# Two-layer hybrid trunk: other order of the first products at each seam, a split norm tile, one operation for the S5 lags, zero matmuls in front

## The chip, the cores and the metric

The kernel runs on one core of a Trainium2 chip. Its time is the device time of one execution in microseconds (us); what is given is the median of three timed executions, 1226.21 us (they were 1229.82, 1226.21 and 1224.89). Engines: PE is TensorE (matrix products and transposes), DVE is VectorE, ACT is ScalarE, POOL is GpSimd, SP is SyncE (here it only issues loads).

## The reference, cut to what matters

256 tokens of width 1024 go through two layers. Each layer is two SwiGLU blocks of hidden width 2816 around a token mixer, then a gated per-layer embedding. Mixer AB of layer 0 is an SSD (16 heads) beside an S5 (64 groups of 16 channels, 64 states each); mixer CD of layer 1 is HGRN2 beside GLA.

```python
for i in range(DEPTH):
    x = layer_norm(a * x + 0.5 * swiglu(x, gate[i, 0], up[i, 0], down[i, 0]), ...)   # LN0 / LN3
    x = layer_norm(a * x + mix(x, ...), ...)                                          # LN1 / LN4
    x = layer_norm(a * x + 0.5 * swiglu(x, gate[i, 1], up[i, 1], down[i, 1]), ...)   # LN2 / LN5
    x = x + sigmoid(x @ ple_gate[i]) * (p[i] @ ple_proj[i])                           # PLE0 / PLE1
```

All of it is float32.

## The kernel before, in words

Products are made in a reduced float32 form on TensorE. Each operand is split in two: `h` is the operand cast (on ACT), `l` is what is left of it (operand minus `h`, on DVE). A product is then three matmuls, `h·wh`, `h·wl` and `l·wh`, added in PSUM. Weights come in units of 1 MB (`Weights.unit`, L45). SP issues the load of a unit into one of two buffers `wst`; ACT casts its halves to `wh_N_0` and `wh_N_1` (L61), DVE subtracts to get `wl_N_0` and `wl_N_1` (L62). A unit serves four blocks k of 128 inputs and 512 outputs, so it feeds 12 matmuls for each of the two token tiles t0 and t1. One product over all 1024 inputs takes two units (kh = 0 and 1) and 24 matmuls for each tile.

The stages follow one another: SwiGLU f00, LN0, mixer AB, LN1, SwiGLU f01, LN2, PLE0, f10, LN3, mixer CD, LN4, f11, LN5, PLE1. In a SwiGLU (`ffn_body`, L198) `gate_up(f)` makes 512 columns (256 of gate, 256 of up) for both tiles, ACT takes the silu, DVE multiplies, PE transposes the result (`ht_f`, L215), and `down` adds to the four accumulators.

A seam is the place where one stage's output becomes the next one's input. At a layer norm (`layer_norm`, L117) DVE scales the tile in two halves of 512 columns (`x_ln`, L138), PE transposes each half in four 128 x 128 pieces into one PSUM tile (`tp_ln`, L142), and `split_xT` (L107) has ACT cast that to `xh` (L112) and DVE subtract to get `xl` (L113). The first product behind a seam is run with `tile_major=True` (`run_tiles`, L163): all 24 matmuls of t0 before those of t1, and for each unit first `h·wh, h·wl` of its four blocks and then its four `l·wh`. This holds for gate_up(0) of every SwiGLU and for the first projection of each mixer (`pj_u` in AB, `pj_hq` in CD). f00's input comes straight from memory: four loads on ACT's queue (L1340), t0's two halves before t1's.

While f00 runs, the parameters of the S5 are also made, one batch b of eight at a time (`s5_params`, L500), mostly on DVE. In `rest` (L534) PE makes the lag matrices in PSUM (`s5k`); DVE writes 16 of the 64 columns of `s5K` (L552) and ACT copies the other 48 (L554), then POOL sends `s5K` to memory.

What sets the order: each engine runs its instructions in one fixed order. That order is chosen when the program is built, by a scheduler that plays the instructions on a timeline of its own; it may put an instruction ahead of ones written earlier. `behind` (L90) adds the demand that an instruction stand after given ones on its engine: `g.w.behind[n]` names the last split of a seam, behind which the casts and subtractions of unit n must stand. PSUM tiles come from a pool in which the tag "tr" (transposes, S5 matrices) has two buffers and "mm" (products) has two. A dependency between two writes or a write and a read of one PSUM tile is kept for the tile as a whole.

Of the kernel before, what the change touches and what calls it, by code (L numbers as in the profile page):

```python
# [8 lines left out]
F32 = mybir.dt.float32  # L9
# [24 lines left out]
def f32(ap):  # L34
    return ap.bitcast(F32)
# [62 lines left out]
def new_xT(g, name):  # L98
    return [g.xt.tile([P, KT, NTOK], F32R, tag=f"x{p}", name=f"x{p}_{name}") for p in "hl"]
# [4 lines left out]
    return [x[:, k, t * P:(t + 1) * P] for x in xT]  # L104


def split_xT(g, t, half, src, xT):  # L107

    nc = g.nc
    s = slice(4 * half, 4 * half + 4)  # L110
    h, l = (x[:, s, t * P:(t + 1) * P] for x in xT)
    a = nc.scalar.copy(h, src)  # L112
    b = nc.vector.tensor_tensor(l, src, f32(h), op=ALU.subtract)  # L113
    g.anchors = a.ins, b.ins


def layer_norm(g, n, t, acc, coef, xT):  # L117

    nc = g.nc
    name = f"ln{n}_{t}"  # L120
    r = g.lnp.tile([P, D], F32, tag="ln_r", name=f"r_{name}")
    st = g.small.tile([P, 2, 6], F32, tag="ln_st", name=f"st_{name}")
    half = [slice(512 * h, 512 * h + 512) for h in range(2)]
    for h in range(2):
        s = half[h]
        op = nc.vector.scalar_tensor_tensor(r[:, s], acc[h], coef, g.x[t][:, s], op0=ALU.mult, op1=ALU.add)
        if t:
            behind(g, op, g.scaled)
        nc.vector.bn_stats(st[:, h, :], r[:, s])
    mv = g.small.tile([P, 2], F32, tag="ln_mv", name=f"mv_{name}")  # L130
    nc.vector.bn_aggr(mv, st.rearrange("p a b -> p (a b)"))
    rstd = rsqrt(g, mv[:, 1:2], 1, EPS / (ALPHA * ALPHA), 1.0, name)
    x = g.xp.tile([P, D], F32, tag=f"x{t}", name=f"x_{name}")
    for h in range(2):
        s = half[h]
        nc.vector.scalar_tensor_tensor(r[:, s], r[:, s], mv[:, 0:1], g.grow[n][0][:, s], op0=ALU.subtract,
                                       op1=ALU.mult)
        op = nc.vector.scalar_tensor_tensor(x[:, s], r[:, s], rstd, g.grow[n][1][:, s], op0=ALU.mult, op1=ALU.add)  # L138
        g.scaled = (op.ins,)
        tp = g.ps.tile([P, 4, P], F32, tag="tr", name=f"tp_{name}_{h}", bufs=2)  # L140
        for k in range(4):
            nc.tensor.transpose(tp[:, k, :], x[:, (4 * h + k) * P:(4 * h + k + 1) * P], g.ident)  # L142
        split_xT(g, t, h, tp, xT)
    g.x[t] = x
    g.w.behind[g.w.at + 1 + t] = g.anchors

# [16 lines left out]
def run_tiles(g, ps, xT, tile_major=False):  # L163

    nc = g.nc

    def part(kh, t, pieces):
        mms = []
        for j in range(4):
            k = 4 * kh + j  # L170
            wh, wl = pieces[j // 2]
            c = slice(512 * (j % 2), 512 * (j % 2) + 512)
            h, l = of_tile(xT, t, k)
            mms += [(h, wh[:, c]), (h, wl[:, c]), (l, wh[:, c])]
        if tile_major:
            mms = [m for i, m in enumerate(mms) if i % 3 < 2] + mms[2::3]
        for i, (x, w) in enumerate(mms):
            nc.tensor.matmul(ps[t], x, w, start=kh == 0 and i == 0, stop=kh == 1 and i == len(mms) - 1)  # L178

    if tile_major:  # L180
        units = [g.w.unit() for kh in range(2)]
        for t in range(NT):
            for kh in range(2):
                part(kh, t, units[kh])
        return
    for kh in range(2):
# [11 lines left out]
def ffn_body(g, name, ln, hooks, hp, wx):  # L198
# [2 lines left out]

    def gate_up(f):
        ps = [g.ps.tile([P, 512], F32, tag="mm", name=f"gu_{name}_{f}_{t}", bufs=2) for t in range(NT)]
        run_tiles(g, ps, g.xT, tile_major=f == 0)
        return ps

    def hidden(f, ps):
# [72 lines left out]
def ple(g, i, pp, out):  # L280
# [16 lines left out]
    def finish(t, c):  # L297
        step = 256 if last and t == NT - 1 and c else 512
        for s in (slice(i, i + step) for i in range(512 * c, 512 * c + 512, step)):
            a = acc[t][c][:, s.start - 512 * c:s.stop - 512 * c]  # L300
            sg = g.pp.tile([P, step], F32, bufs=2, tag="ple_sg", name=f"sg_ple{i}_{t}_{s.start}")
            nc.scalar.activation(sg, a, AF.Tanh, scale=0.5)
            nc.vector.scalar_tensor_tensor(sg, sg, 1.0, pp[t][:, s], op0=ALU.add, op1=ALU.mult)
            nc.vector.scalar_tensor_tensor(xn[t][:, s], sg, 0.5, xn[t][:, s], op0=ALU.mult, op1=ALU.add)
            if last:
                nc.sync.dma_start(out[t * P:(t + 1) * P, s], xn[t][:, s])
        if last:
            return
        tp = g.ps.tile([P, 4, P], F32, tag="tr", name=f"tp_ple{i}_{t}_{c}", bufs=2)
        for k in range(4):  # L310
            nc.tensor.transpose(tp[:, k, :], xn[t][:, (4 * c + k) * P:(4 * c + k + 1) * P], g.ident)
        split_xT(g, t, c, tp, xT)

    for kh in range(2):
        units[0][kh] = g.w.unit()
# [184 lines left out]
def s5_params(g, b, half):  # L500
# [34 lines left out]
    def rest():  # L535
# [242 lines left out]
def ssd_steps(g, pool, raw):  # L778
# [529 lines left out]
def tile_trunk(ctx: ExitStack, tc: tile.TileContext, xnat, xTd, pT, lnr, colsd, cstd, abrow, abdt, s5bc, cdlr, cdgu,  # L1308
# [23 lines left out]
    g.s5T = [g.dram.tile([P, 4, 64], F32, tag=f"s5T{b}", name=f"s5T{b}") for b in range(NB)]  # L1332
    g.perm = [[g.dram.tile([512, NTOK] if n == "u" else [32, 16, NTOK], F32, tag=f"{n}{c}", name=f"{n}dram{c}")
               for c in range(2)] for n in "uy"]
    g.xT = new_xT(g, "in")
    for t in range(NT):
        xs = g.lnp.tile([P, KT, P], F32, tag="ln_r", name=f"xin_{t}")
        for h in range(2):
            s = slice(4 * h, 4 * h + 4)
            nc.scalar.dma_start(xs[:, s], xTd[t][:, s])  # L1340
            split_xT(g, t, h, xs[:, s], g.xT)

    def load_constants():
        cs = g.const.tile([P, cstd.shape[1]], F32, tag="cst", name="cs")
# [92 lines left out]
def constants():  # L1437
# [4 lines left out]
    for lv in range(7):  # L1442
# [101 lines left out]
```

## Time and profile before

| | |
|---|---|
| median of three timed executions | 1226.21 us |
| profiled execution, its own time | 1226.01 us |
| its span, first to last instruction | 1224.2 us |
| PE busy | 1189.6 us (97%) |
| DVE busy | 852.3 us (70%) |
| ACT busy | 588.5 us (48%) |
| mean granted TensorE clock | 0.994 of full speed |
| chain of waits | PE 67%, DVE 10%, DMA 2%, ACT 2% |

The profiled execution lasts 1.8 us longer than its span, and lies 0.2 us under the median, so times worked out against it need no correction. Stages by time in the span: f00 to 218, AB to 442, f01 to 632, PLE0 to 662, f10 to 852, CD to 1000, f11 to 1195, PLE1 to the end. In the rows, a line such as `PE L178 MATMUL gu_f<-wh,xh_in` is the product into `gu_f` of line 178; a trailing bracket gives how long the engine idled before the instruction and which work ended the wait.

### The profile page before, as it was taken

The page shows a single profiled execution, that of the slowest core. Times are in us where ns is not written, and L with a number is a line of the kernel's source. Part 1 is how long each engine was busy: PE and PEld are TensorE (multiplying, and loading weights), DVE is VectorE, ACT ScalarE, POOL GpSimd, SP SyncE. Part 2 cuts the span into 40 slices and gives each one's busy share as a digit, 9 for nine tenths or more (in the row PEclk, how much of TensorE's full clock was granted, in tenths as well). Part 3 has the DMA queues.
Part 4 walks back from the last instruction along what each step waited for, and adds up shares of the span by engine and source line. Part 5 has one row for each costly group of instructions (what it writes and reads, how often), then busy time and mean ns, then how long its engine had stood idle before and what let it go on. Part 6 is the DMA issues. An engine that isn't in the chain of part 4 may idle for free.

```text
span 1224.2 us, 17248 instructions
## 1 busy us (share of the span) xinstructions
PE 1189.6 (97%) x6786; PEld 987.4 (81%) x6786; DVE 852.3 (70%) x1352; ACT 588.5 (48%) x870; POOL 73.2 (6%) x126
## 2 busy tenths in 40 slices
PE   8999999999999999999999999999999999999998
PEld 6887777798878878888887888887888868888886
DVE  6999874779999675554576545456689876555566
ACT  5644443444666434444434444443575535444434
POOL 0011112120212000000000000000100100000000
PEclk9999999899999999999999999999999999999999
DMA  7567667587744546555526555554633327555532
GB/s 282 207 228 257 223 205 290 211 271 239 198 122 143 192 153 226 201 176 194 203 95 240 196 190 188 185 193 158 241 113 128 104 99 254 176 202 174 203 138 103
DMA packets 44609, 232.74 MB, mean 190 GB/s; under 512 B 9680, under 2 KB 10352, under 8 KB 20848
## 3 DMA queue, kind: packets, MB, share of 16 engines
q1 hardware_dynamic: 30672, 206.06, 48.5%
q0 software_dynamic: 4688, 14.16, 3.7%
q10 hardware_dynamic: 9168, 11.42, 2.9%
q8 instruction: 53, 0.87, 0.3%
q14 instruction: 28, 0.23, 0.1%
HBM read 219.56 MB, written 12.06 MB: 189 GB/s over the span
## 4 chain that ended last, share of the span: by engine, by line
PE 67%; DVE 10%; DMA 2%; ACT 2%; issue 1%; ACTq 0%; DVEq 0%
PE gu_f L178 29%; PE acc_f L72 5%; PE acc_f L70 5%; PE acc_f L71 5%; DVE wl L62 3%; DMA wst<-in_wall_dram 1%; PE acc_ab L72 1%; PE acc_ab L70 1%; PE acc_ab L71 1%; PE ht_f L215 1%; PE pj_u L178 1%; PE pj_hg L178 1%; PE pj_gr L178 1%; PE pj_hi L178 1%; PE pj_gv L178 1%
## 5 line engine op out<-in xcount | busy, mean ns | idle before, releaser
L62 DVE TENSOR_TENSOR wl<-wst,wh 128x1024 fp32r<-128x1024 f32 (+1 forms) x378 | 453.0, 1217 | 258.2 <-ACT wh L61 251.0
L61 ACT CAST wh<-wst 128x1024 fp32r<-128x1024 f32 (+1 forms) x378 | 385.9, 1045 | 349.2 <-PE acc_f L72 104.6
L70 PE MATMUL acc_f<-wh,hh_f 128*128 128x512 f32 x352 | 137.3, 391 | 1.9 <-ACT wh L61 1.4
L71 PE MATMUL acc_f<-wl,hh_f 128*128 128x512 f32 x352 | 137.5, 392 | 0.0
L72 PE MATMUL acc_f<-wh,hl_f 128*128 128x512 f32 x352 | 135.2, 392 | 0.0
L70 PEld LDWEIGHTS acc_f<-wh,hh_f 128*128 128x128 f32 x352 | 66.1, 188 | 15.8 <-ACT wh L61 1.6
L178 PE MATMUL gu_f<-wh,xh_in 128*128 128x512 f32 x176 | 71.9, 413 | 6.0 <-ACT wh L61 6.0
L72 PEld LDWEIGHTS acc_f<-wh,hl_f 128*128 128x128 f32 x352 | 66.1, 188 | 13.7
L71 PEld LDWEIGHTS acc_f<-wl,hh_f 128*128 128x128 f32 x352 | 66.1, 188 | 13.5
L178 PE MATMUL gu_f<-wh,xh_ple 128*128 128x512 f32 x176 | 70.8, 402 | 2.6 <-ACT xh_ple L112 2.6
L178 PE MATMUL gu_f<-wh,xh_ab 128*128 128x512 f32 x176 | 69.8, 396 | 0.5 <-ACT xh_ab L112 0.5
L178 PE MATMUL gu_f<-wl,xh_in 128*128 128x512 f32 x176 | 70.2, 402 | 0.0
L178 PE MATMUL gu_f<-wl,xh_ab 128*128 128x512 f32 x176 | 68.8, 391 | 1.3 <-DVE wl L62 1.3
L178 PE MATMUL gu_f<-wh,xh_cd 128*128 128x512 f32 x176 | 69.9, 397 | 0.0
L178 PE MATMUL gu_f<-wl,xh_ple 128*128 128x512 f32 x176 | 69.6, 396 | 0.0
L178 PE MATMUL gu_f<-wl,xh_cd 128*128 128x512 f32 x176 | 68.8, 391 | 0.7 <-DVE wl L62 0.7
L211 ACT ACTIVATE sg_f<-gu_f 128x256 f32<-128x256 f32 x88 | 33.7, 383 | 69.1 <-PE gu_f L178 67.8
L178 PE MATMUL gu_f<-wh,xl_ab 128*128 128x512 f32 x176 | 66.9, 391 | 0.0
L178 PE MATMUL gu_f<-wh,xl_cd 128*128 128x512 f32 x176 | 66.8, 391 | 0.0
L178 PE MATMUL gu_f<-wh,xl_ple 128*128 128x512 f32 x176 | 66.7, 391 | 0.0
L178 PE MATMUL gu_f<-wh,xl_in 128*128 128x512 f32 x176 | 66.6, 392 | 0.0
L212 DVE TENSOR_TENSOR sg_f<-sg_f,gu_f 128x256 f32<-128x256 f32 x88 | 36.8, 418 | 27.8 <-ACT sg_f L211 27.7
(469 smaller groups left out, 2348.9 us busy)
## 6 DMA issues: line engine op xcount, KB each, us to landing
wst<-in_wall_dram SPq DMA_DIRECT2D x185, 1024.0 KB, 4.8
row<-in_lnr_dram SPq DMA_DIRECT2D x12, 512.0 KB, 6.4
s5d<-s5pk POOLq DMA_DIRECT2D x8, 704.0 KB, 4.3
tab<-s5d ACTq DMA_DIRECT2D x8, 384.0 KB, 4.7
Q<-s5d ACTq DMA_DIRECT2D x8, 320.0 KB, 4.5
wst<-in_wall_dram SPq DMA_DIRECT2D x4, 512.0 KB, 6.7
s5d<-s5W POOLq DMA_DIRECT2D x8, 256.0 KB, 2.5
W<-s5d ACTq DMA_DIRECT2D x8, 256.0 KB, 4.0
```

The costliest lines, as they stand in the source:

```text
L61: ops = [nc.scalar.copy(wh[:, c], src[:, c])]
L62: ops.append(nc.vector.tensor_tensor(wl[:, c], src[:, c], f32(wh[:, c]), op=ALU.subtract))
L70: nc.tensor.matmul(out, xh, wh, start=first, stop=False)
L71: nc.tensor.matmul(out, xh, wl, start=False, stop=False)
L72: nc.tensor.matmul(out, xl, wh, start=False, stop=last)
L178: nc.tensor.matmul(ps[t], x, w, start=kh == 0 and i == 0, stop=kh == 1 and i == len(mms) - 1)
L211: nc.scalar.activation(sg, ps[t][:, 0:256], AF.Silu)
L212: nc.vector.tensor_tensor(sg, sg, ps[t][:, 256:512], op=ALU.mult)
L215: nc.tensor.transpose(tp[:, k, :], sg[:, k * P:(k + 1) * P], g.ident)
```

## The change: what it does

1. Start. Eleven matmuls of a zeroed 128 x 128 tile with itself (128 x 512 out, results not used) stand in front of the first product. x is loaded half by half (t0 and t1 of the first half, then of the second). f00's first gate_up is no longer tile-major.
2. Seams. The tile-major order is now, for each tile: `h·wh, h·wl` of blocks 0 to 3, `h·wh` of blocks 4 to 7, all eight `l·wh`, and last `h·wl` of blocks 4 to 7. This holds for f01, f10 and f11 and for `pj_u` and `pj_hq`.
3. Layer norm. For the first half of t0 the scaling (`x_ln`), the transposes and the split run in two pieces of 256 columns, in the same PSUM tile as before.
4. S5. All 64 lag columns are made by one DVE operation (the constant `fold` grows from 16 to 64 columns); the eight ACT copies go.
5. PLE0. The splits of the units 100 and 101 (the first two of f10) must stand behind the split of the second half of t0 and of t1.

```diff
+START_MMS = 11
...
-def split_xT(g, t, half, src, xT):
+def split_xT(g, t, half, src, xT, part=slice(0, 4)):
-    s = slice(4 * half, 4 * half + 4)
+    s = slice(4 * half + part.start, 4 * half + part.stop)
...
-        op = nc.vector.scalar_tensor_tensor(x[:, s], r[:, s], rstd, g.grow[n][1][:, s], op0=ALU.mult, op1=ALU.add)
-        g.scaled = (op.ins,)
         tp = g.ps.tile([P, 4, P], F32, tag="tr", name=f"tp_{name}_{h}", bufs=2)
-        for k in range(4):
-            nc.tensor.transpose(tp[:, k, :], x[:, (4 * h + k) * P:(4 * h + k + 1) * P], g.ident)
-        split_xT(g, t, h, tp, xT)
+        n = 4 if t or h else 2
+        for k0 in range(0, 4, n):
+            c = slice((4 * h + k0) * P, (4 * h + k0 + n) * P)
+            op = nc.vector.scalar_tensor_tensor(x[:, c], r[:, c], rstd, g.grow[ln][1][:, c], op0=ALU.mult, op1=ALU.add)
+            g.scaled = (op.ins,)
+            for k in range(k0, k0 + n):
+                nc.tensor.transpose(tp[:, k, :], x[:, (4 * h + k) * P:(4 * h + k + 1) * P], g.ident)
+            split_xT(g, t, h, tp[:, k0:k0 + n, :], xT, slice(k0, k0 + n))
...
-        if tile_major:
-            mms = [m for i, m in enumerate(mms) if i % 3 < 2] + mms[2::3]
...
         for t in range(NT):
-            for kh in range(2):
-                part(kh, t, units[kh])
+            mms = [[], [], []]
+            for k in range(KT):
+                wh, wl = units[k // 4][k % 4 // 2]
+                c = slice(512 * (k % 2), 512 * (k % 2) + 512)
+                h, l = of_tile(xT, t, k)
+                mms[0].append((h, wh[:, c]))
+                if k < 4:
+                    mms[0].append((h, wl[:, c]))
+                else:
+                    mms[2].append((h, wl[:, c]))
+                mms[1].append((l, wh[:, c]))
+            mms = sum(mms, [])
+            for i, (x, w) in enumerate(mms):
+                nc.tensor.matmul(ps[t], x, w, start=i == 0, stop=i == len(mms) - 1)
...
-        run_tiles(g, ps, g.xT, tile_major=f == 0)
+        run_tiles(g, ps, g.xT, tile_major=f == 0 and name != "f00")
...
         split_xT(g, t, c, tp, xT)
+        if c:
+            g.w.behind[g.w.at + 1 + t] = g.anchors
...
-        nc.vector.scalar_tensor_tensor(K[:, 48:64], g.cst("fold"), g.cols("s5d")[:, b:b + 1], kp[:, 0:16], op0=mul,
-                                       op1=add)
-        nc.scalar.copy(K[:, 64:112], kp[:, 16:64])
+        nc.vector.scalar_tensor_tensor(K[:, 48:112], g.cst("fold"), g.cols("s5d")[:, b:b + 1], kp, op0=mul, op1=add)
...
+    busy = g.const.tile([P, P], F32R, tag="busy", name="busy")
+    nc.vector.memset(f32(busy), 0.0)
+    ps = g.ps.tile([P, 4, P], F32, tag="tr", name="busy_ps", bufs=2)
+    for i in range(START_MMS):
+        nc.tensor.matmul(ps, busy, bc(busy, 1, 4), start=True, stop=True)
     g.xT = new_xT(g, "in")
-    for t in range(NT):
-        xs = g.lnp.tile([P, KT, P], F32, tag="ln_r", name=f"xin_{t}")
-        for h in range(2):
+    xs = [g.lnp.tile([P, KT, P], F32, tag="ln_r", name=f"xin_{t}") for t in range(NT)]
+    for h in range(2):
+        for t in range(NT):
             s = slice(4 * h, 4 * h + 4)
-            nc.scalar.dma_start(xs[:, s], xTd[t][:, s])
-            split_xT(g, t, h, xs[:, s], g.xT)
+            nc.scalar.dma_start(xs[t][:, s], xTd[t][:, s])
+            split_xT(g, t, h, xs[t][:, s], g.xT)
```

How the built order moves is shown at three places. First ACT behind LN3, from the casts of t0 on. `tp_ln3_0_0` is the transposed first half of t0, `tp_ln3_0_1` the second; `wh_133_*` is the second unit of `pj_hq`, `nws_glr` a small weight that comes by a load of its own. Before:

```order
L112 CAST xh_f10_7743<-tp_ln3_0_0_7784 128x4x128
L112 CAST xh_f10_7743<-tp_ln3_0_1_7793 128x4x128
L61 CAST wh_133_0_7881<-wst_133_7879 128x1024
L61 CAST wh_133_1_7885<-wst_133_7879 128x1024
L1238 DMA gup_8124<-in_cdgu_dram 32x256
L595 CAST nws_glr_8102<-nw_glr_8100 128x8x16
L1055 COPY ev_hq_0_7937<-pj_hq_0_7867 128x512
```

and now:

```order
L113 CAST xh_f10_7758<-tp_ln3_0_0_7798 128x2x128
L113 CAST xh_f10_7758<-tp_ln3_0_1_7810 128x4x128
L62 CAST wh_133_0_7899<-wst_133_7897 128x1024
L62 CAST wh_133_1_7903<-wst_133_7897 128x1024
L1252 DMA gup_8142<-in_cdgu_dram 32x256
L609 CAST nws_glr_8120<-nw_glr_8118 128x8x16
L113 CAST xh_f10_7758<-tp_ln3_0_0_7798 128x2x128
L1069 COPY ev_hq_0_7955<-pj_hq_0_7885 128x512
```

The cast of the first half has become two of 256 columns. The second of them stands behind both `wh_133` casts and `nws_glr`, five rows after the first. At LN0, LN1 and LN4 it likewise stands behind both `wh` casts of the second unit (34, 62 and 151); `nws` is in between at LN3 alone.

Next PE at the same place, from the transposes of t0 on. `wh_132_*` and `wl_132_*` are the first unit of `pj_hq`, which serves blocks 0 to 3. Before:

```order
L142 MATMUL tp_ln3_0_0_7784<-cs_217,x_ln3_0_7781 128x128 x4
L142 MATMUL tp_ln3_0_1_7793<-cs_217,x_ln3_0_7781 128x128 x4
L178 MATMUL pj_hq_0_7867<-wh_132_0_7871,xh_f10_7743 128x512
L178 MATMUL pj_hq_0_7867<-wl_132_0_7872,xh_f10_7743 128x512
L178 MATMUL pj_hq_0_7867<-wh_132_0_7871,xh_f10_7743 128x512
L178 MATMUL pj_hq_0_7867<-wl_132_0_7872,xh_f10_7743 128x512
L178 MATMUL pj_hq_0_7867<-wh_132_1_7875,xh_f10_7743 128x512
L178 MATMUL pj_hq_0_7867<-wl_132_1_7876,xh_f10_7743 128x512
L178 MATMUL pj_hq_0_7867<-wh_132_1_7875,xh_f10_7743 128x512
L178 MATMUL pj_hq_0_7867<-wl_132_1_7876,xh_f10_7743 128x512
L178 MATMUL pj_hq_0_7867<-wh_132_0_7871,xl_f10_7744 128x512 x2
```

and now:

```order
L146 MATMUL tp_ln3_0_0_7798<-cs_231,x_ln3_0_7796 128x128 x2
L146 MATMUL tp_ln3_0_1_7810<-cs_231,x_ln3_0_7796 128x128 x4
L198 MATMUL pj_hq_0_7885<-wh_132_0_7889,xh_f10_7758 128x512
L198 MATMUL pj_hq_0_7885<-wl_132_0_7890,xh_f10_7758 128x512
L198 MATMUL pj_hq_0_7885<-wh_132_0_7889,xh_f10_7758 128x512
L198 MATMUL pj_hq_0_7885<-wl_132_0_7890,xh_f10_7758 128x512
L146 MATMUL tp_ln3_0_0_7798<-cs_231,x_ln3_0_7796 128x128 x2
L198 MATMUL pj_hq_0_7885<-wh_132_1_7893,xh_f10_7758 128x512
L198 MATMUL pj_hq_0_7885<-wl_132_1_7894,xh_f10_7758 128x512
L198 MATMUL pj_hq_0_7885<-wh_132_1_7893,xh_f10_7758 128x512
L198 MATMUL pj_hq_0_7885<-wl_132_1_7894,xh_f10_7758 128x512
L198 MATMUL pj_hq_0_7885<-wh_133_0_7899,xh_f10_7758 128x512 x2
```

Two of the four transposes of the first half now stand behind four products. In the program as built they also wait for DVE's subtraction `xl` of the first piece, since both pieces share one PSUM tile; the four products after them need the second piece of `xh`.

Last ACT between PLE0 and f10. `tp_ple0_T_H` is the transposed half H of tile T, `wh_100_*` and `wh_101_*` the first two units of f10. Before:

```order
L61 CAST wh_100_0_6441<-wst_100_6439 128x1024
L302 ACTIVATE sg_ple0_0_512_6366<-acc_ple0_0_1_6227 128x512
L61 CAST wh_100_1_6445<-wst_100_6439 128x1024
L61 CAST wh_101_0_6521<-wst_101_6519 128x1024
L112 CAST xh_ple0_6230<-tp_ple0_0_0_6304 128x4x128
L112 CAST xh_ple0_6230<-tp_ple0_1_0_6315 128x4x128
L302 ACTIVATE sg_ple0_1_512_6401<-acc_ple0_1_1_6229 128x512
L61 CAST wh_101_1_6525<-wst_101_6519 128x1024
L112 CAST xh_ple0_6230<-tp_ple0_0_1_6370 128x4x128
L61 CAST wh_102_0_6555<-wst_102_6553 128x1024
```

and now:

```order
L316 ACTIVATE sg_ple0_0_512_6381<-acc_ple0_0_1_6242 128x512
L113 CAST xh_ple0_6245<-tp_ple0_0_0_6319 128x4x128
L113 CAST xh_ple0_6245<-tp_ple0_1_0_6330 128x4x128
L316 ACTIVATE sg_ple0_1_512_6416<-acc_ple0_1_1_6244 128x512
L113 CAST xh_ple0_6245<-tp_ple0_0_1_6385 128x4x128
L62 CAST wh_100_0_6456<-wst_100_6454 128x1024
L62 CAST wh_100_1_6460<-wst_100_6454 128x1024
L113 CAST xh_ple0_6245<-tp_ple0_1_1_6420 128x4x128
L62 CAST wh_101_0_6536<-wst_101_6534 128x1024
L62 CAST wh_101_1_6540<-wst_101_6534 128x1024
```

Before, three of the four `wh` casts of the units 100 and 101 stand ahead of the first `xh_ple`; now three `xh_ple` stand ahead of all of them, and `wh_100` follows the split of t0's second half.

## Rows read from the trace of the kernel before

**Rows 1.** The page's first part: busy us, share of the span, instructions.

```profile
PE 1189.6 (97%) x6786; PEld 987.4 (81%) x6786; DVE 852.3 (70%) x1352; ACT 588.5 (48%) x870; POOL 73.2 (6%) x126
```

**Rows 2.** Waits of PE: line waited for, us in total, times, longest.

```profile
PE gu_f L178 <- ACT wh L61: 6.0, 1, 6.0
PE tp_ln L142 <- DVE x_ln L138: 3.5, 3, 1.7
PE gu_f L178 <- ACT xh_ple L112: 2.6, 1, 2.6
PE gu_f L178 <- DVE wl L62: 2.1, 2, 1.3
PE pj_z L178 <- DVE bc L817: 1.9, 1, 1.9
PE ht_f L215 <- ACT s5K L554: 1.8, 2, 1.5
...
PE pj_hq L178 <- DVE wl L62: 1.6, 1, 1.6
```

**Rows 3.** Windows: length, busy us by engine, PEclk, DMA share, GB/s.

```profile
21.10:50.00 28.90, 28.90 (x133) 23.81 (x132) 24.34 (x71) 22.30 (x35) 0.00 (x0) 1.00 0.66 223
...
222.00:245.00 23.00, 22.07 (x119) 19.04 (x119) 16.73 (x23) 14.68 (x19) 1.58 (x2) 0.87 0.71 256
...
665.00:668.50 3.50, 3.50 (x10) 2.76 (x9) 3.50 (x6) 1.48 (x3) 0.00 (x0) 0.52 0.29 122
```

**Rows 4.** Timeline of the start: start us, us, engine, line, operation [idle before].

```profile
6.03 0.79 PE L178 MATMUL gu_f<-wh,xh_in 128*128 128x512 f32 x1 [6.03 <-ACT wh L61]
...
10.45 0.63 PE L178 MATMUL gu_f<-wh,xh_in 128*128 128x512 f32 x1
...
10.87 0.63 PE L178 MATMUL gu_f<-wl,xh_in 128*128 128x512 f32 x1
...
15.21 1.16 DVE L62 TENSOR_TENSOR wl<-wst,wh 128x1024 fp32r<-128x1024 f32 x1
...
21.11 0.48 PE L178 MATMUL gu_f<-wh,xh_in 128*128 128x512 f32 x1
```

**Rows 5.** Timeline of the S5 wait inside f00.

```profile
105.80 0.23 DVE L552 SCALAR_TENSOR_TENSOR s5K<-cs,lc,s5k 128x16 f32<-128x16 f32 x1
105.94 0.42 DVE L218 TENSOR_TENSOR hl_f<-ht_f,hh_f 128x256 fp32r<-128x256 f32 x1
...
106.36 0.33 PE L215 MATMUL ht_f<-cs,sg_f 128*128 128x128 f32 x1 [1.49 <-ACT s5K L554]
```

**Rows 6.** Timeline of the first product behind LN1, PE.

```profile
450.77 1.03 PE L142 MATMUL tp_ln<-cs,x_ln 128*128 128x128 f32 x8
```

**Rows 7.** Timeline between PLE0 and f10, ACT and PE.

```profile
663.03 1.04 ACT L61 CAST wh<-wst 128x1024 fp32r<-128x1024 f32 x1 [3.42 <-DMA wst<-in_wall_dram]
663.98 1.07 ACT L112 CAST xh_ple<-tp_ple 128x512 fp32r<-128x512 f32 x2
...
664.61 0.50 PE L178 MATMUL gu_f<-wh,xh_ple 128*128 128x512 f32 x1 [2.61 <-ACT xh_ple L112]
```

**Rows 8.** Timeline behind LN3, PE and ACT.

```profile
853.51 0.50 PE L178 MATMUL pj_hq<-wh,xh_f 128*128 128x512 f32 x1 [0.24 <-ACT xh_f L112]
...
858.37 0.50 PE L178 MATMUL pj_hq<-wl,xh_f 128*128 128x512 f32 x1 [1.60 <-DVE wl L62]
...
861.22 1.04 PE L142 MATMUL tp_ln<-cs,x_ln 128*128 128x128 f32 x8
...
853.83 2.01 ACT L61 CAST wh<-wst 128x1024 fp32r<-128x1024 f32 x2
857.30 0.30 ACT L595 CAST nws_glr<-nw_glr 128x128 fp32r<-128x128 f32 x1 [1.45 <-DMA nw_glr<-in_cdlr_dram]
```

**Rows 9.** Timeline behind LN4, PE.

```profile
1001.71 0.50 PE L178 MATMUL gu_f<-wh,xh_cd 128*128 128x512 f32 x1
...
1009.04 1.29 PE L142 MATMUL tp_ln<-cs,x_ln 128*128 128x128 f32 x8 [0.26 <-DVE x_ln L138]
```

More of the change, by code (lines that the diff above doesn't have):

```diff
@@ L114, in split_xT, with layer_norm @@
     g.anchors = a.ins, b.ins
-def layer_norm(g, n, t, acc, coef, xT):
+def layer_norm(g, ln, t, acc, coef, xT):
     nc = g.nc
-    name = f"ln{n}_{t}"
+    name = f"ln{ln}_{t}"
     r = g.lnp.tile([P, D], F32, tag="ln_r", name=f"r_{name}")
@@ L135, in layer_norm @@
         s = half[h]
-        nc.vector.scalar_tensor_tensor(r[:, s], r[:, s], mv[:, 0:1], g.grow[n][0][:, s], op0=ALU.subtract,
+        nc.vector.scalar_tensor_tensor(r[:, s], r[:, s], mv[:, 0:1], g.grow[ln][0][:, s], op0=ALU.subtract,
                                        op1=ALU.mult)
-        op = nc.vector.scalar_tensor_tensor(x[:, s], r[:, s], rstd, g.grow[n][1][:, s], op0=ALU.mult, op1=ALU.add)
-        g.scaled = (op.ins,)
         tp = g.ps.tile([P, 4, P], F32, tag="tr", name=f"tp_{name}_{h}", bufs=2)
-        for k in range(4):
-            nc.tensor.transpose(tp[:, k, :], x[:, (4 * h + k) * P:(4 * h + k + 1) * P], g.ident)
-        split_xT(g, t, h, tp, xT)
+        n = 4 if t or h else 2
[6 more added lines that the diff above has]
+            split_xT(g, t, h, tp[:, k0:k0 + n, :], xT, slice(k0, k0 + n))
     g.x[t] = x
@@ L782, in ssd_steps @@
     for t in range(NT):
-        nc.tensor.matmul(ps[:, t, :], raw[:, t * P:(t + 1) * P], g.cst("fold")[0:32, :], start=True, stop=True)
+        nc.tensor.matmul(ps[:, t, :], raw[:, t * P:(t + 1) * P], g.cst("fold")[0:32, 0:16], start=True, stop=True)
     row = pool.tile([P, 48], F32, tag="abrow", name="abrow", bufs=1)
@@ L1292, in mixer_cd @@
         out_project(g, "cd", parts, ln, 1.0 / ALPHA, tail=2)
-CST = {"ident": 128, "incl": 128, "strict": 128, "mask3": 384, "cidx": 16, "levels": 448, "fold": 16, "half": 2}
+CST = {"ident": 128, "incl": 128, "strict": 128, "mask3": 384, "cidx": 16, "levels": 448, "fold": 64, "half": 2}
 COLS = {"conv": 80, "ssdw": 8, "bglu": 8, "s5v": 96, "s5d": NB, "halfpi": 1, "lb": 8, "glab": 2}
@@ L1448, in constants @@
              np.broadcast_to(np.concatenate([np.arange(8), np.arange(0, 64, 8)]).astype(np.float32), (P, 16)), *levels,
-             (j[:, None] % 16 == np.arange(16)[None, :]).astype(np.float32),
+             (j[:, None] % 16 == np.arange(64)[None, :]).astype(np.float32),
              (j[:, None] // 64 == np.arange(2)[None, :]).astype(np.float32)]
```

## The prediction

> **What bounds the kernel now.** I read the page's shares first: PE is busy 1189.6 of 1224.2 us, so whatever happens on the other engines, only some 35 us of PE's idle time and the stretches of slow clock can move the end [rows 1]. The waits of PE then tell where that idle time lies: 6.0 us at the start, 3.5 us for `x_ln` at three layer norms, 2.6 us behind PLE0, 2.1 us (1.3 at LN1, about 0.7 at LN4) and 1.6 us (LN3) for the weights' low parts `wl`, 1.8 us for the S5 copy on ACT, 1.9 us for a constant in AB [rows 2]. The windows show what a matmul costs: 133 of them in 28.90 us, 0.22 us each with the clock whole (some are short transposes, so I use 0.228 for a 128 x 512 product), and ten in 3.50 us at a granted clock of 0.52, so 1.75 us lost in that stretch [rows 3]. The change touches nearly all these waits and nothing else on PE's path, except that the order inside AB is built anew. So the sum goes seam by seam. It is made against the profiled execution, 1226.0 us with its 1.8 us around the span, which stands 0.2 us under the median, so the result is the forecast of the median as well.
>
> **Start.** Before, the first product starts at 6.03; products follow 0.42 apart (10.45, 10.87), twice the steady distance, and the next column block (gate_up 1, tile t0) starts at 21.11 [rows 4]. The zero matmuls need no data: eleven at 0.42 us fill 4.6 us, which fits before 6.03 if they can start by 1.4 us. If they bring the clock up, the first real products run at 0.228, but then they wait for supply: the last `wl` of unit 1 is done at 15.21 + 1.16 = 16.37 [rows 4]. At that point 11 of the 24 matmuls of the unit are left (one tile's second half less one, the other tile's second half): 16.6 + 11 × 0.228 + 0.36 for two transposes is 19.45. That is 1.7 us less than 21.11. If the clock stays slow until 13 as before, nothing is gained; with x's last half landing a little earlier too I would not go over 2.5. Term −1.7, range 0 to −2.5. The zero matmuls add no path of their own: they end before the first operands are there.
>
> A page of the Trainium skill bears on this, "TensorE: Matmul & The Clock Gate", section "What's actually happening": the default clock is the slow one, and activity releases it. By that rule the zero matmuls do their work and the term is −1.7; no run here shows yet whether zeros count as activity.
>
> **S5 in f00.** The 1.8 us of waits stand at two places, 1.49 us of it at 106.36, where `ht_f` needs a transpose buffer that the ACT copy of `s5K` frees; that copy comes after DVE's 16 columns at 105.80 [rows 2, 5]. One DVE operation of 64 columns lies between the 0.23 us of 128x16 and the 0.42 us of 128x256 [rows 5]; I take 0.28, nearest the first, so +0.05 each for eight, beside DVE work that PE does not wait for. The copy and its hand-over (105.80 + 0.23 to 106.36, 0.3 us) go, and batch 1's operation now stands ahead of five rows of S5 work on DVE. I take −1.2 of the 1.8; DVE is 84% busy already from 21 to 50 [rows 3], and one of its subtractions may come late elsewhere. Range −1.8 to +1.
>
> **Layer-norm seams.** Here lies the question. The new order puts the eight `h·wl` of the second unit last, so PE no longer waits for `wl`: that is worth 1.3 at LN1, 1.6 at LN3 and 0.7 at LN4 [rows 2]. The first piece of 256 columns lets the first product start some 0.4 to 0.7 earlier (half of a 0.7 us scaling, and a shorter cast). But blocks 2 and 3 need the second piece of `xh`, which ACT casts only after both `wh` casts of the second unit. At LN3 these took 2.01 us [rows 8]. At LN3 `nws_glr` stands in between as well, and its load landed only at 857.30 [rows 8].
>
> - LN3. First product at 853.1 instead of 853.51. Four products run to 854.0; then PE waits with two pieces of work left to it (transposes) until `nws_glr` (857.30 + 0.30) and the second piece (0.37) are cast, 858.05. Behind that stand 20 matmuls, 4.55 us: t0 ends at 862.6, where before t1's transposes started at 861.22 [rows 8]. Loss 1.4.
> - LN4. First product 1001.0 instead of 1001.71 [rows 9]; four products, then the second half's transposes and cast (to 1003.2), two `wh` casts (2.01), the second piece: 1005.5. 20 matmuls end at 1010.1. DVE must also bring the second `xl` piece, behind two scalings and two `wl`, at about 1008 to 1009, which costs 0.6 to 1.4 more. Against 1009.04 [rows 9] the loss is 1.7 (bounds 1.1 and 2.4).
> - LN1. The same without delays of DVE: stall to 445.7, t0 ends at 450.3 where before 450.77 stood [rows 6]. Gain 0.4.
> - LN0. The same count: a wait of 3.4 us for the second piece, but the first product 0.7 earlier and, in before, a slow clock already (0.87 over 23 us, 6 us at half speed [rows 3]), part of which the wait now covers. t0 ends 0.9 earlier if the clock is whole after the wait, 0.5 later if not. I take −0.2.
>
> Each of the waits at LN3 and LN4 is about 2.5 to 2.8 us long. The row nearest is PLE0's wait of 2.61 us: right behind it comes the window with clock 0.52 [rows 3, 7]; the wait of 1.60 at LN3 was followed by matmuls at full pace (858.37 to 861.22: 11 matmuls in 2.85 us) [rows 8]. So I add one slow stretch of 1.7 us to each: LN3 +3.1, LN4 +3.4. Without it they are +1.4 and +1.7.
>
> LN2 and LN5 change by the split alone, and their products behind do not wait: 0.
>
> **PLE0 to f10.** Before, ACT cast `xh_ple` at 663.98, after a `wh` cast that had waited 3.42 us for its load; PE started at 664.61, having waited 2.61 us, and ran at 0.52 of the clock in the window to 668.5 [rows 3, 7]. Its 48 matmuls of two tiles and eight transposes (0.9) so ended at 664.61 + 48 × 0.228 + 0.9 + 1.75 = 678.2. Now the `xh_ple` of both tiles' first halves come before, so PE goes on at 661.9 with the first unit's products. It then waits for t0's second half (cast at 666.1 to 666.7) and for `wh_100` behind it (668.7): 1.35 + 0.5. The same count gives 661.9 + 10.95 + 0.9 + 1.85 = 675.6. Term −2.6; if the slow stretch comes all the same −0.9; if nothing waits −4.4 (all of the idle time and the slow stretch).
>
> A rule of the Trainium skill speaks against this change, on the same page ("Architectural detail"): ACT and DVE take their instructions strictly in order, while PE may pull weight loads ahead. The trace agrees at PLE0, where ACT kept the finished transposes waiting behind a `wh` cast that itself waited for its load [rows 7]. By the rule the second piece cannot pass the `wh` casts, and the losses at LN3 and LN4 stand; an ACT that passed them would leave the seams with their gains, which is the first rival's time.
>
> **AB.** The scheduler has put some ten groups of instructions there in another order. The waits that could move are the 1.9 us for a constant, with a slow stretch of 1.75 behind it, and a few of about 1 us [rows 2, 3]. I see no direction in it: 0, range −3 to +3.
>
> **Sum.** −1.7 − 1.2 − 0.2 − 0.4 + 3.1 + 3.4 − 2.6 = +0.4: 1226.4 us.
>
> **Rivals.**
> - Faster: the second piece is no bar. For: the products need it only after four others. Against: the built order, and the trace's PLE0. Then LN3 gains 1.6 and LN4 0.7 with 0.4 each for the earlier start: −1.7 − 1.2 − 0.2 − 0.4 − 2.0 − 1.1 − 2.6 = −9.2, 1216.8 us. The forecast with AB at its good end (−3) and no slow stretches (−3.4) comes to 1220.0, the same side.
> - Slower: the waits behind the four layer norms bring two slow stretches each, as in before at LN0, where a wait of 1.7 us [rows 2] went with 6 us at half speed [rows 3]. That is 1.75 more at LN3 and LN4 and 1.75 at LN1, with 1.6 at LN0 (its one end against the 0.2 gained, and a second stretch in part): +0.4 + 3.5 + 1.75 + 1.6 = +7.3, 1233.3 us. It decides from a wait of about 1.7 us on, if that is followed by another short one. For: LN0's row. Against: PLE0's longer wait cost one stretch.
> - The start does not do what it says: zeros don't raise the clock, or DVE, which f00's S5 work fills, takes back the lead. Then 1.7 on the forecast, 1228.1; that does not leave the band.
>
> **How the numbers follow.** A measurement of this kernel can tell about 0.5%, 6.1 us, from no change; that is the bound of the three chances. The forecast, with the third rival (0.10 of it), holds 0.64; the faster rival with the good ends of AB and the clocks 0.22; the slower one 0.14. The likeliest case alone is good for 1221 to 1230 (the clocks −3.4, S5 and AB ±3, PLE0 ±1.7). The range for 8 in 10 takes a part of each rival: 1217 to 1232. Faster 0.22, same 0.64, slower 0.14.
>
> **What would show it.** After the change, PE's waits should hold no `wl` at the layer norms, but waits for ACT's `xh` of 2 to 3 us behind LN0, LN3 and LN4, with the clock at about half behind LN3 and LN4; the second piece of `xh` on ACT directly after the `wh` casts. gate_up 1 of f00 should start near 19.5; `ht_f` should wait no more than 0.6 for `s5K`; behind PLE0 no wait at 661.9, and the clock should be whole. The forecast is wrong if the waits for the second piece are shorter than 1 us, or if the stages' ends drift by over 3 us inside f00 or AB.

## The result, and the profile after

The changed kernel is slower: 1241.6 us median (four timed executions, 1237.62 to 1246.1) against 1225.76 us of the kernel before beside it; ratio 1.0116, 95% interval [1.0092, 1.0141]. The profiled execution has a span of 1238.7 us against 1224.2, 14.5 us more. The median lies outside the forecast range.

PE's waits after (line waited for, us in total, times, longest), to be read against [rows 2]:

```profile
PE tp_ln L146 <- DVE x_ln L143: 3.7, 3, 1.6
PE gu_f L198 <- ACT xh_cd L113: 3.1, 3, 2.4
PE pj_hq L198 <- ACT xh_f L113: 2.7, 3, 2.2
PE acc_f L71 <- ACT wh L62: 2.2, 1, 2.2
PE seg L853 <- DVE cr L894: 1.9, 2, 1.4
PE xs L1016 <- ACT xsT L833: 1.7, 1, 1.7
PE gu_f L198 <- ACT xh_ab L113: 1.6, 2, 1.3
PE s5y L736 <- DVE S L721: 1.5, 1, 1.5
...
PE pj_u L198 <- ACT xh_f L113: 1.1, 2, 0.8
...
PE ht_f L229 <- DVE s5K L568: 0.9, 1, 0.9
```

The 6.0 us at the start, the waits for `wl` at the layer norms and the 2.6 us behind PLE0 are gone. In their place stand waits for ACT's `xh` behind LN1, LN3 and LN4, as forecast, and longer waits of `seg`, `xs` and `s5y` inside AB, which were not. Two signs of the forecast did not come: at LN0 the wait for the second piece (`pj_u`) is 0.8 where 2 to 3 us were named, and `ht_f` waits 0.9 for `s5K` where at most 0.6 was.

Where the 14.5 us come from is read by the starts of the same PE instruction in both traces. The columns give how much later each comes than in before, in us (less is earlier); every kernel is told of below. A column is one execution, and those of one program scatter (e3: 1227.15 to 1238.27 us), the slower ones mostly at a lower granted clock (e3: 0.997 down to 0.987), so a difference of 1.7 or 3.4 us in one cell can be a stretch of slow clock and not the edit.

| place | after | e1 | e3 | e6 | e9 | e10 | e11 |
|---|---|---|---|---|---|---|---|
| f00, gate_up 1 | −1.2 | −1.3 | −1.5 | −1.7 | −0.1 | −0.2 | −1.7 |
| f00, gate_up 6 | −2.3 | −2.0 | −2.1 | −1.5 | −0.4 | −0.2 | −0.9 |
| f00, gate_up 8 | +0.6 | +1.0 | +0.8 | +1.8 | −0.4 | −0.2 | +5.0 |
| f00, last product | +0.9 | +1.2 | +1.1 | +3.0 | −1.2 | −0.6 | +6.5 |
| pj_u, tile t1 (LN0 passed) | +1.6 | +1.6 | +0.4 | +3.1 | −1.0 | −1.6 | +6.7 |
| AB, last product | +6.5 | +1.5 | +6.0 | +7.7 | −1.6 | −1.0 | +11.2 |
| f01, tile t1 (LN1 passed) | +6.0 | +0.5 | +5.1 | +7.7 | −2.5 | −2.0 | +10.3 |
| PLE0, last product | +6.3 | +0.5 | +5.1 | +7.6 | −2.6 | −2.0 | +10.3 |
| f10, last product | +4.4 | −1.4 | +3.2 | +4.9 | −4.5 | −3.9 | +8.4 |
| pj_hq, tile t1 (LN3 passed) | +8.1 | −2.4 | +2.2 | +4.9 | −5.5 | −4.9 | +7.4 |
| CD, last product | +9.7 | −2.3 | +5.4 | +4.9 | −5.1 | −1.7 | +7.5 |
| f11, tile t1 (LN4 passed) | +13.9 | −2.4 | +5.3 | +4.9 | −5.1 | −1.0 | +7.3 |
| last | +14.1 | −2.6 | +5.3 | +4.9 | −5.2 | −1.2 | +7.2 |

For the changed kernel this gives, place by place: start −1.2, the rest of f00 +2.1, LN0 +0.7, AB +4.9, LN1 −0.5, PLE0 −1.9, LN3 +3.7, CD +1.6, LN4 +4.2; the other 0.4 lie between. LN3 in its trace, PE and then ACT:

```profile
858.47 0.40 PE L198 MATMUL pj_hq<-wl,xh_f 128*128 128x512 f32 x1
859.31 0.44 PE L146 MATMUL tp_ln<-cs,x_ln 128*128 128x128 f32 x2 [0.45 <-DVE xl_f L114]
861.95 0.80 PE L198 MATMUL pj_hq<-wh,xh_f 128*128 128x512 f32 x1 [2.20 <-ACT xh_f L113]
862.54 0.63 PE L198 MATMUL pj_hq<-wl,xh_f 128*128 128x512 f32 x1
...
857.99 2.00 ACT L62 CAST wh<-wst 128x1024 fp32r<-128x1024 f32 x2
861.33 0.30 ACT L609 CAST nws_glr<-nw_glr 128x128 fp32r<-128x128 f32 x1 [1.33 <-DMA nw_glr<-in_cdlr_dram]
861.53 0.37 ACT L113 CAST xh_f<-tp_ln 128x256 fp32r<-128x256 f32 x1
```

The transposes of the second piece end at 859.75; its cast is ready to go, but ACT first casts `wh` and then waits for `nws_glr`. PE stands 2.20 us, and the matmuls behind run at 0.43 each (862.54 to 862.97), where the same stretch behind LN3 ran whole before [rows 8]. The windows behind LN3 and around LN4 (length, busy by engine, PEclk, DMA share, GB/s):

```profile
862.00:870.00 8.00, 8.00 (x27) 6.39 (x28) 3.23 (x5) 0.47 (x1) 3.34 (x5) 0.64 0.72 246
1010.00:1024.00 14.00, 10.99 (x40) 8.36 (x40) 10.35 (x18) 3.86 (x7) 0.94 (x1) 0.76 0.25 77
```

Granted clocks of 0.64 and 0.76 are 2.9 of 8 us and 3.4 of 14 us lost. At LN4 that is two slow stretches: products from 1011.00 start 0.43 apart, those from 1016.70 0.23, those from 1017.99 to 1020.98 again 0.43.

### The profile page after: what moved, and what is told of

Same layout as the page of the kernel before. It is cut to its first block, busy times and chain, and to the rows that moved or that the text cites. A ratio compares the mean times of both kernels' runs of the same rounds, so it can differ in the third digit from the quotient of the medians.

```text
span 1238.7 us, 17266 instructions
## 1 busy us (share of the span) xinstructions
PE 1200.9 (97%) x6797; PEld 993.1 (80%) x6797; DVE 856.4 (69%) x1365; ACT 586.8 (47%) x866; POOL 72.7 (6%) x126
## 5 line engine op out<-in xcount | busy, mean ns | idle before, releaser
L180 PE MATMUL gu_f<-wh,xh_ple 128*128 128x512 f32 x160 | 63.4, 396 | 0.0
L180 PE MATMUL gu_f<-wh,xh_ab 128*128 128x512 f32 x160 | 63.3, 396 | 0.0
L180 PE MATMUL gu_f<-wh,xh_cd 128*128 128x512 f32 x160 | 63.3, 396 | 0.0
L180 PE MATMUL gu_f<-wh,xl_ab 128*128 128x512 f32 x160 | 62.5, 391 | 0.0
L180 PE MATMUL gu_f<-wh,xl_cd 128*128 128x512 f32 x160 | 62.5, 391 | 0.0
L180 PE MATMUL gu_f<-wh,xl_ple 128*128 128x512 f32 x160 | 62.4, 390 | 0.0
L180 PE MATMUL gu_f<-wl,xh_ab 128*128 128x512 f32 x160 | 62.3, 390 | 0.0
L180 PE MATMUL gu_f<-wl,xh_cd 128*128 128x512 f32 x160 | 62.3, 390 | 0.0
L180 PE MATMUL gu_f<-wl,xh_ple 128*128 128x512 f32 x160 | 62.3, 389 | 0.0
```

## The experiments

**e1, no split.** All of the change but part 3.

```diff
-        n = 4 if t or h else 2
+        n = 4
```

> All of the change but the norm split: the first half of t0 is one piece again at every layer norm. In the changed kernel the loss against before lies, by the starts of the same PE instructions, in f00 (+2.1 us after a start that gains 1.3), LN0 (+0.7), AB (+4.9), LN3 (+3.7), CD (+1.6) and LN4 (+4.2). Theory: the second piece of xh, cast behind both wh casts, costs LN3 and LN4, and the split at LN0 makes the scheduler order AB anew, which costs the 4.9. Then all three vanish here, the wl waits are gone too (1.6 at LN3, 0.7 at LN4, 1.3 at LN1), the start, f00 and PLE0 stay as in the changed kernel: 1219 to 1223 us. Rival 1: the new matmul order at the seams (h.wl of the second unit last) is what costs at LN3 and LN4: then they still lose 8 us together, about 1232. Rival 2: AB's new order comes from the S5 operation or the start: AB still loses 4.9, about 1227.

Measured: 1225.76 against 1227.16, ratio 0.9992 [0.9974, 1.001]; span 1221.7. By the table LN3 gains 1.0 (after: loses 3.7) and LN4 is even (after: loses 4.2), AB is as before, f00 still loses. The matmul order alone costs nothing at LN3 and LN4, and LN1 and LN3 gain; rival 1 falls. Rival 2 falls only for the two parts together with the new seams: alone, each of them reorders AB (e5 and e6). The median is above the theory's 1219 to 1223; the profiled execution (1223.48) is the fastest of the ten and lies just above it.

**e2 and e3, the split at some seams.** e2 at every layer norm but LN0, e3 at LN0 alone.

```diff
-        n = 4 if t or h else 2
+        n = 4 if t or h or ln == 0 else 2    # e2
+        n = 4 if t or h or ln else 2         # e3
```

> The changed kernel with the split at every layer norm but LN0. Theory (the split at LN0 reorders AB, the splits at LN3 and LN4 make the waits): AB as in the kernel without any split, LN3 and LN4 lose 3.7 and 4.2 as in the changed kernel: about 1230 to 1235, 8 above the kernel without split. Rival (AB's loss has another cause): about 1240, as the changed kernel.

> The changed kernel with the split at LN0 alone. Theory: AB in the order of the changed kernel, so +5 to +6 at LN0 and AB against the kernel without split, no waits for a second piece at LN1, LN3 and LN4: about 1225 to 1229. Rival (AB's loss has another cause than the split at LN0): as the kernel without split, 1219 to 1223, or, if LN3 and LN4 lose by the matmul order, 1232 and more.

Measured: e2 1236.62 (forecast up to 1235), ratio 1.0069 [1.0042, 1.0097]; e3 1233.48, ratio 1.0043 [1.0018, 1.0068]. In e3 AB loses 5.6 us and LN3 and LN4 lose nothing. In e2 AB loses 1.2, LN3 2.4 and LN4 4.7. So the losses at LN3 and LN4 come with the split there, and with the other parts in place AB's 5 us come when the split stands at LN0, whose place is ahead of AB in the program. Both are above their ranges. In e2's profile f00 ends 4.0 us later than before, in the order of the changed kernel, with two slow stretches (granted clock 0.83 from 125 to 135 us and 0.84 from 185 to 196), and CD loses 3.1; e3's CD loses 3.2 with an order that is that of e1.

**e4, the second piece ahead of wh.**

```diff
+    anchors = []
...
             split_xT(g, t, h, tp[:, k0:k0 + n, :], xT, slice(k0, k0 + n))
+            anchors += g.anchors
-    g.w.behind[g.w.at + 1 + t] = g.anchors
+    g.w.behind[g.w.at + 1 + t] = tuple(anchors)
```

> The changed kernel, but the wh and wl of the second unit must stand behind both pieces of the first half, so that ACT casts the second piece before wh. Theory (the wait is for ACT's order): at LN4 the wait of 2.4 us for xh falls under 1 and the clock stays whole there, which gives back 3 to 4 us; LN1 gives back about 1; LN3 gives nothing, since there the second piece still stands behind the cast of nws_glr, whose load lands some 4 us after the seam. AB is ordered anew once more (unknown, +-3). About 1236. Rival (the wait is for the transposes, held back by the subtraction xl on DVE, not for ACT's order): LN4's wait stays over 2 us, about 1240.

Measured: 1236.7, ratio 1.0082 [1.0053, 1.0111], 1236 being forecast. LN4 loses 0.9 in place of 4.6, counted from f11's first product to tile t1's. The trace of e4 at LN4, PE and then ACT:

```profile
1010.63 1.03 PE L147 MATMUL tp_ln<-cs,x_ln 128*128 128x128 f32 x6
1012.17 0.50 PE L200 MATMUL gu_f<-wh,xh_cd 128*128 128x512 f32 x1 [0.51 <-ACT xh_cd L113]
...
1011.26 0.86 ACT L113 CAST xh_cd<-tp_ln 128x512 fp32r<-128x512 f32 x2 [1.72 <-PE tp_ln L147]
1012.01 2.01 ACT L62 CAST wh<-wst 128x1024 fp32r<-128x1024 f32 x2
```

The same work with the order of the changed kernel:

```profile
1012.81 1.48 PE L146 MATMUL tp_ln<-cs,x_ln 128*128 128x128 f32 x6
1016.70 0.50 PE L198 MATMUL gu_f<-wh,xh_cd 128*128 128x512 f32 x1 [2.41 <-ACT xh_cd L113]
...
1013.90 0.59 ACT L113 CAST xh_cd<-tp_ln 128x512 fp32r<-128x512 f32 x1 [2.95 <-PE tp_ln L146]
1014.38 1.99 ACT L62 CAST wh<-wst 128x1024 fp32r<-128x1024 f32 x2
1016.28 0.37 ACT L113 CAST xh_cd<-tp_ln 128x256 fp32r<-128x256 f32 x1
```

With the two `wh` casts behind the second piece the wait falls from 2.41 to 0.51. So it is ACT's order, not the transposes. The total agrees with the forecast in part by luck. LN3 loses 2.2 and not the 3.7 that the theory left it, and the demand costs where no product had waited: from f01's to PLE0's last product e4 loses 3.5, at LN2, with waits of 0.8 for `xl` and 0.8 for `wl` and a granted clock of 0.89 from 640 to 655, and at LN5 the same two waits come again (1.9 from f11's last product to the end). In the changed kernel these places cost 0.2 each.

**e5 and e6, the S5 part alone and the start alone.** e5 is before with the one DVE operation; e6 is before with the eleven zero matmuls, x half by half and f00's first product not tile-major.

```diff
+        nc.vector.scalar_tensor_tensor(K[:, 48:112], g.cst("fold"), g.cols("s5d")[:, b:b + 1], kp, op0=mul, op1=add)  # e5
+    for i in range(START_MMS):                                                             # e6, with the x loads
+        nc.tensor.matmul(ps, busy, bc(busy, 1, 4), start=True, stop=True)
```

> The kernel before with the S5 part alone (one DVE operation of 64 columns, no ACT copies). Theory: the loss of 2.9 us between gate_up 6 and gate_up 8 of f00, which stood alike in the changed kernel and in all four variants so far, comes from this part: batch 2's products s5k now stand where DVE is behind, and PE waits for s5K and for hl. Then f00's last product ends 1 to 2.5 us later than before. AB has a third order here (350 rows of PE's differ from before), worth -2 to +5. Total 1226 to 1233. Rival: the loss in f00 comes from the start (all of f00's work is ahead by 1.3 us and DVE cannot follow): then f00 ends here 1 to 1.7 us earlier than before, since the wait of 1.5 us for the ACT copy is gone: 1224 to 1228.

> The kernel before with the start alone (zero matmuls, x half by half, f00's first product not tile-major). Theory: 1.3 us are gained at gate_up 1 and are kept to the end of f00; AB has a fourth order (338 rows of PE's differ), worth -2 to +5: 1224 to 1230. Rival (DVE bounds f00): the gain is lost again between gate_up 6 and 8, f00 ends as before or later.

Measured: e5 1231.14, ratio 1.0048 [1.0029, 1.0066]; e6 1231.43, ratio 1.0042 [1.002, 1.0064]. My theory on f00 falls: e5 ends f00 0.4 us earlier than before, and e6 loses 3.4 between gate_up 6 and 8, so that loss comes with the start, as e6's rival had it. In e6 AB loses 4.6; in e5 4.1, behind an f00 that lost nothing, so AB's loss isn't carried over from f00. e5's total is in its theory's range, but for another reason: AB and a CD that loses 3.1 in its profile.

**e7, the PLE0 part alone.**

```diff
+        if c:
+            g.w.behind[g.w.at + 1 + t] = g.anchors
```

> The kernel before with the PLE0 part alone; the order is that of before everywhere else. Theory: -2.0 us at the first product of f10, the slow clock there gone, all of it kept to the end: ratio 0.998 to 0.999. Rival (a gain at a seam is given back later, since the loads are the bound of f10): nothing is left at the end.

Measured: 1224.18 against 1225.73, ratio 0.9986 [0.9965, 1.0006]. In the profile f10's first product comes 2.2 us earlier and f10's end 3.1 (−3.8 against −0.7 at PLE0's end). The profiled execution then loses 1.5 at LN3 and 3.1 in CD, where the built order is that of before; parts of both ran at half clock there (0.76 from 855 to 862 us, 0.89 from 915 to 945). The mechanism held; the interval does not exclude no change.

**e8, neither split nor S5.** The split undone as in e1, the S5 lines as before.

> The change without the norm split and without the S5 part. Theory: the kernel without split, with f00 back at the start's gain (f00's last product 1.3 to 2.5 us earlier than there), AB in almost the order of the start alone (32 rows differ): 1220 to 1226 by what that order is worth. Rival (the start costs f00 what it gains): f00 as in the kernel without split, 1225 to 1230.

Measured: 1231.63, ratio 1.0044 [1.0022, 1.0066]. The rival is right on f00, which loses 3.2 between gate_up 6 and 8; the total is above both ranges, since AB loses 7.3 in an order almost that of e6. With all three of start, S5 and seams (e1) AB's built order happened to fall back on that of before.

**e9 to e11, zero matmuls by number.** As e8, with none, four and six zero matmuls.

```diff
-START_MMS = 11
+START_MMS = 4      # e10; 6 in e11; in e9 the loop is left out
```

> The change without the norm split, the S5 part and the zero matmuls; x still comes half by half, f00's first product is not tile-major, the seams have the new order and PLE0 its new demand. The built order of f00 and AB is that of before but for 28 and 32 rows of PE. Theory (the zero matmuls, a first wait of the scheduler's own timeline, are what reorders f00 and AB; seams and PLE0 gain): f00 ends as before or up to 1 us earlier, AB as before, LN1 and LN3 give 0.9 to 1.0 each, PLE0 2.2 to 3.8: 4 to 6 us faster than before, 1219 to 1222. Rival (loading x half by half or the first product's order costs f00 its 3 us): f00 ends 2 us later than before, 1224.

> As e9 with four zero matmuls in front. The order of f00 and AB differs from e9's by no row but these four. Theory: f00 and AB as in e9, the clock at the start comes up a little sooner or not at all, 0 to 1 us gained: 1218 to 1222. Rival (zero matmuls delay the work itself, not the scheduler's order): f00 or AB lose 2 us or more.

> As e10 with six zero matmuls; nothing else in the program is written in another way, but f00 (120 rows of PE's) and AB (338 rows) come out in the other order, the one of the start alone. Theory (it is the order): f00 loses about 3 us after gate_up 6 and AB 5 to 8, so 1227 to 1231, some 8 above four zeros. Rival (something else in the earlier kernels costs AB its time): within 2 us of four zeros.

Measured: e9 1222.29, ratio 0.9978 [0.9959, 0.9997]; e10 1226.02, ratio 1.0 [0.9987, 1.0013]; e11 1231.02, ratio 1.0038 [1.0022, 1.0054]. e11 is at the top of its forecast, e9 0.3 above its own, while e10 missed its 1218 to 1222 by 4. Between e10 and e11 stand two matmuls of 0.4 us that hold up nobody, and the other built order. By the table e11 loses 7.4 after gate_up 6 of f00 and 4.5 in AB, and e10 gains 0.4 and loses 0.6. Of the 7.4 some 3.4 are two slow stretches (granted clock 0.83 from 125 to 135 us and 0.84 from 185 to 196), which leaves about 4. The medians lie 5.0 us apart, not 8, and the slowest e10 (1228.34) is faster than the fastest e11 (1228.5): that is what the two orders of f00 and AB are worth together. PE's waits in AB's last part, e10:

```profile
PE s5y L738 <- DVE S L723: 1.0, 1, 1.0
PE seg L855 <- ACT E L857: 0.7, 1, 0.7
PE seg L855 <- DVE cr L896: 0.7, 1, 0.7
```

and e11:

```profile
PE s5y L738 <- DVE S L723: 2.1, 1, 2.1
PE seg L855 <- DVE cr L896: 1.9, 2, 1.4
PE cp L894 <- ACT E L857: 0.8, 1, 0.8
PE cp L894 <- DVE x0d L878: 0.8, 1, 0.8
PE yp L892 <- DVE xd L875: 0.7, 1, 0.7
```

The windows from about the first `glu` product to the first of `acc_ab`, e10 and e11:

```profile
348.00:396.40 48.40, 45.24 (x399) 40.08 (x398) 44.86 (x103) 30.14 (x65) 8.99 (x16) 1.00 0.46 134
```

```profile
352.00:408.00 56.00, 48.45 (x404) 41.03 (x403) 49.98 (x109) 30.29 (x64) 10.02 (x15) 1.00 0.37 114
```

Nearly the same products (399 and 404 records) take 7.6 us more in these windows, 7.2 by the starts of the products themselves; PE idles 7.6 in place of 3.2. In e10, 33 of the first 48 `glu` products run before the first `yp` of the SSD and 15 more between its small products (`yp`, `seg`, `cp`), while these wait for DVE and ACT; in e11 all 48 run ahead, and nothing is left to fill the waits. Against before, e11's stretch is 7.1 us longer, the one ahead of it, with `pj_z` and `xs`, 3.1 shorter and the one behind 0.4 longer, so AB's sum is 4.5. That the order makes the loss is shown by e10 and e11; that it does so by these unfilled waits is read from the traces and has no run of its own.

e9 is the fastest kernel here, below before by an interval that just excludes no change. e10 shares its order, but its median is 3.7 us higher. Its profile lost 3.2 us in CD, where one stretch ran slow; whether that is what parts the medians stays open. e9's and e10's windows there:

```profile
915.00:945.00 30.00, 30.00 (x192) 25.40 (x191) 29.18 (x53) 16.63 (x27) 0.00 (x0) 1.00 0.32 106
```

```profile
915.00:945.00 30.00, 30.00 (x178) 25.28 (x177) 27.71 (x50) 14.29 (x24) 0.00 (x0) 0.89 0.30 103
```

PE is busy all through both, and e10's clock is 0.89.

## Why the prediction was wrong

The direction of the two largest seam terms was right. The sum was wrong, mainly because two terms of built order were taken for nothing: AB at 0, and f00 behind the start. In the order of the forecast:

- **Start**: gain 1.2, forecast 1.7. The zeros do bring the clock up (11 in 4.22 us from 1.09; the first real product at 6.17 takes 0.50, where [rows 4] show 0.79). In e9, without the zeros, the first products stay at half clock as before. That answers the open point of the forecast: zeros count as activity here.
- **f00**: forecast −1.2, measured +2.1. The step that failed is to count the S5 copy's wait as gone while the order beside it is new. The wait at 106 went, but f00 loses 2.9 between gate_up 6 and 8: there PE now waits 0.9 for `s5K`, which DVE reaches late, and 0.5 each for `hh_f` and `hl_f`. DVE after, and the PE instruction that waits:

```profile
123.67 1.22 DVE L63 TENSOR_TENSOR wl<-wst,wh 128x1024 fp32r<-128x1024 f32 x1
124.81 0.27 DVE L568 SCALAR_TENSOR_TENSOR s5K<-cs,lc,s5k 128x64 f32<-128x64 f32 x1
...
125.13 0.44 PE L229 MATMUL ht_f<-cs,sg_f 128*128 128x128 f32 x2 [0.89 <-DVE s5K L568]
```

  The 64 columns cost 0.27, as taken. But alone the S5 part is worth 0.4 at f00's end (e5), not 1.2, and loses nothing there; e6, e10 and e11 show that the start's zeros choose the order that loses. The third rival, that f00's DVE takes back the lead, came nearest; it was priced at 1.7, and f00's term is 3.3 off.
- **AB**: forecast 0, −3 to +3; measured +4.9. This is the step that failed most: I saw the new order, gave it no sign and put the term at nothing. (The slow stretch that the forecast names there is in none of its rows; the trace has it, with a granted clock of 0.96 from 300 to 340 us.) It did not put the result outside the range by itself: 1241.6 less 4.9 is 1236.7, and only with f00's 3.3 and CD's 1.6 gone as well would it come under 1232. e1, e3, e6 and e8 show AB as before in the old order and 4.6 to 7.3 us slower in the new ones; e10 and e11 show it between two programs that differ by two idle matmuls. Four new orders came out (e5's, e6's with e8's and e11's, the changed kernel's with e3's, and e4's) and every one was slower, by 4.1 to 7.3 us. That the order before was an uncommonly good one, so that a shuffle should have been priced as a loss, is a guess from these four; f00 has a counter-example, e5's new order there, which lost nothing.
- **LN3 and LN4**: forecast +3.1 and +3.4, measured +3.7 and +4.2. The mechanism is the one forecast, the second piece behind `wh` (e1 and e4). That the sizes come so near is partly luck. Each term was a loss by the wait (1.4 and 1.7) and one slow stretch of 1.7. By the two windows some 3 us went to the clock at each place (part of LN4's first slow stretch fell into the wait), which leaves about 1 us each for the wait: the clock was priced too low and the wait too high. At LN4 the first slow stretch began at 1011.00, ahead of the wait of 2.41, and a slow stretch stands there in the profiles of e5, e7 and e10 as well (0.86 from 1000 to 1012), which have no split. So it isn't shown that the wait called it.
- **LN1**: −0.5, forecast −0.4. **LN0**: +0.7, forecast −0.2 with ends at −0.9 and +0.5; the wait of 3.4 us counted for the second piece was 0.8. **PLE0**: −1.9, forecast −2.6; the waits came to 1.8 in sum, as counted, 0.4 of it at the first product, where none was expected, and 1.4 for `wh`.
- **CD**: forecast nothing, measured +1.6, a slow stretch at 936 us. Such a one came in the profiled executions of the changed kernel, e2, e3, e5, e7 and e10, and not in those of before, e1, e4, e6, e8, e9 and e11, among them pairs with the same order there (e9 and e10; before and e7). What decides it stays open.

The slower rival (1233 us, two slow stretches behind each layer norm) was the right side and right on the clock at LN3 and LN4, but not at LN1 (−0.5) and only in part at LN0 (+0.7). The rest came from AB and CD, which no rival held, and from f00, which only the third did.

## What to carry to other kernels

Where a scheduler orders all engines over a whole program, read the built order of the stages that an edit does not touch: a piece ahead of them, even an idle matmul, can reorder them. Here all four new orders of AB were slower, and two of three of f00. Undo parts by place as well as by kind (the split at one seam, zeros by number); two programs that differ in one harmless thing and in the order separate the order's price from the edit's. A tile cut in two to start a product earlier must be checked on the strictly ordered engine that serves it: the second piece needs a place ahead of the long operations that follow the first. Ask for that place only at the seams where a product waits for it: at LN2 and LN5 the same demand cost e4 3.5 and 1.9 us.

## What the runs showed of the hardware

The length of a wait did not settle whether the slow clock followed. It followed PE's wait of 2.6 behind PLE0 [rows 7] and the one of 2.20 at LN3 in the changed kernel, but not one of 2.24 in f00 of the same execution, after which the window from 186 has a granted clock of 1.00:

```profile
185.98 0.74 PE L71 MATMUL acc_f<-wh,hh_f 128*128 128x512 f32 x2 [2.24 <-ACT wh L62]
186.00:194.00 8.00, 8.00 (x35) 6.36 (x36) 5.85 (x7) 3.96 (x6) 0.54 (x1) 1.00 0.78 259
```

And the wait of 1.60 at LN3, which full pace followed in before [rows 8], came again in e7 with the same order, and there the slow clock followed:

```profile
854.54 0.50 PE L182 MATMUL pj_hq<-wl,xh_f 128*128 128x512 f32 x1 [1.60 <-DVE wl L63]
855.00:862.00 7.00, 6.79 (x27) 5.14 (x26) 3.59 (x6) 2.99 (x5) 1.25 (x2) 0.76 0.79 276
```

In CD it came between 920 and 940 us with no idle time of PE at all: 30.00 busy of 30.00 us and a granted clock of 0.89 in e10. So a stretch at 1.2 GHz isn't always the trace of a wait, and it moves single executions of one program by some 3 us (CD in e9 and e10, which have one order there, against before: 0.4 and 3.2 us lost). The forecast priced one slow stretch behind a wait like PLE0's 2.6 and none behind one like LN3's 1.6; each had one row to stand on, and these rows don't bear it out.
